# RWKV-7 value stores of a hybrid decoder step: issued from GpSimd's queue instead of ScalarE's

## The chip, the core and the metric

The kernel runs on one core of one Trainium2 chip. The metric is the device time of one execution in microseconds (us), the median of several runs. The core's engines are TensorE (PE in the profile; its weight loads are PEld), VectorE (DVE), ScalarE (ACT), GpSimd (POOL) and SyncE (SP). Each works through its own instructions in order; waits between them are semaphores. A DMA is issued by an instruction in the queue of one of these engines; ACTq and SPq in the profile are the instructions of ScalarE's and SyncE's sequencers.

## The reference: one step of a two-layer decoder

1024 prompt tokens and 8 sequences of 8 sample tokens (1088 columns in all, model width 1024) go through two layers. Layer 0 mixes tokens by stick-breaking attention, layer 1 by RWKV-7 with 16 heads of 64; each mixer is followed by a squared-ReLU MLP of width 4096. Cut to the part that matters here:

```python
r = xr @ w_r
k = xk @ w_k
v = xv @ w_v
...
def step(S, inp):
    r_t, w_t, k_t, v_t, kk_t, b_t = inp
    sa = jnp.einsum('bhij,bhj->bhi', S, kk_t)
    S = (S * w_t[:, :, None, :] - sa[..., None] * b_t[:, :, None, :]
         + v_t[..., None] * k_t[:, :, None, :])
    return S, jnp.einsum('bhij,bhj->bhi', S, r_t)
```

`v` is needed twice: with features first (for the bonus term) and, for the chunked form of the recurrence, with tokens first, per head and chunk of 64 tokens.

## The kernel before

Activations lie with the 1024 features on partitions, in eight tiles of 128, and tokens along the free dimension. The tokens are cut into two halves (`HALF`): the first has 576 prompt tokens, in matmul chunks of 288, the second 448 prompt and 64 sample tokens in one chunk of 512. `dense` (L354 to L368) multiplies in three passes for precision: weights and activations are split into a high and a low part (`weight`, L350 and L351; `split`), and per tile of weights three matmuls (L364 to L366) add into one PSUM bank. PE does this during almost the whole kernel.

Beside this main line runs background work: attention, then the RWKV units (`rw_units`, `rw_unit`: per eighth of the features, decay, key normalisation, and the small matrices of all chunks) and then the RWKV chains (`rw_chain`), which walk the recurrence. The background is a Python generator, and `step` (L186), called after each three matmuls, takes pieces of it at a set rate. `beside` adds a second such stream (for example the loads and splits of the next projection). So the program order interleaves main line and background, and the framework (`TileContext` with `schedule_with_timeline_sim=True`) fixes each engine's final order when the program is built, from a planner's model of costs. The framework also gives the DMAs their landing semaphores.

The value projection of layer 1 is the third `dense_to` of `mixer_in` (L1685). For each of eight feature tiles m:

- `dense` makes 128 features of v for the half, and `self.copy` (L132 on ScalarE or L134 on VectorE, alternating by `flip`) brings them from PSUM (`dq`) to SBUF (`dn`).
- ScalarE issues the store of `dn` to `s_vt` (L1017).
- `rw_value` (L1021) transposes `dn` on PE (L140) into PSUM (`vq`) with tokens on partitions, copies it to SBUF (`vt`, again L132 or L134), and stores it to the scratch `s_v` in pieces: for each head of the pair and each group of 64 partitions one DMA. A block of 512 tokens gives four stores of 64 KB, the last 64 tokens of the first half two stores of 16 KB. That is 6 x 8 = 48 stores in the first half and 4 x 8 = 32 in the second, all issued from ScalarE's queue.

`dn`, `vt` and many other tiles share the six buffers of the pool `n`; a buffer can be written again when the last DMA that reads it has landed.

During the two value stages the background is `rw_unit`. On ScalarE it has, among others, activations (L1093 `s` and `a`, L1106 `G`, L1107 `Gi`, L1117 `t`), copies (L1169 `L`, L1184 `S`) and the DMA issues of its results to `s_st`, `s_p` and `s_l` (L1124, L1144, L1173, L1174, L1187, L1188, L1189). On GpSimd it has L1105 (memset of `G`), L1108 (`gend`), L1119 and L1120 (`a`), and L1130 (`AR`, second part), which L1188 stores. Every second `split` puts its low part on GpSimd too (L311: `xlo`, `slo`), and `residual` adds the sample columns there (L385). `rw_chain` reads `s_v` back on SyncE's queue (L1274), `rw_samples` at L1389. SyncE issues all weight loads of these stages (L347) and most other loads. GpSimd issues no DMA in this kernel.

Of the kernel before, what the change touches and what calls it, by code (L numbers as in the profile page):

```python
# [106 lines left out]
class Kern:  # L107
# [913 lines left out]
    def rw_value(self, m, pt, t, tmp, ps):  # L1021

        nc = self.nc
        for w0 in range(0, pt.W, 512):
            n = min(128, pt.W - w0)
            nw = min(512, pt.W - w0) // n
            q = ps.tile([128, 512], F32, tag="dps", name="vq")
            for i in range(nw):
                self.transpose(q[:n, 128 * i:128 * i + 128], t[:, w0 + 128 * i:w0 + 128 * i + n])
            o = tmp.tile([128, 4, 128], F32, tag="n", name="vt")[:n, :nw, :]  # L1030
            self.copy(o, q[:n, :128 * nw].rearrange("p (w c) -> p w c", w=nw))
            c = pt.c0 + w0 // 64
            for hd in range(2):
                for p in range(n // 64):
                    nc.scalar.dma_start(self.s_v[m, hd][:, c + p:c + p + 2 * nw - 1:2, :],
                                      o[64 * p:64 * p + 64, :, 64 * hd:64 * hd + 64])

    def rw_keys(self, m, pt, k, pp, ps):
# [747 lines left out]
```

## Time and profile before

| | |
|---|---|
| time, median of 3 runs | 3655.77 us (3653.04 to 3656.8) |
| profiled execution | 3661.88 us |
| its span, first to last instruction | 3660.2 us |
| mean granted PE clock | 0.972 |
| value stage of the first half, s_v issues | 1585.0 to 1712.9 us |
| value stage of the second half, s_v issues | 2448.0 to 2546.5 us |

The profile is one execution. A row of the waits view names who waited and for whom, then the total in us, the times and the longest. A timeline row has the start, the length, engine, line, operation, output and inputs, and in brackets how long the engine had been idle and what ended it. In the table by stretch each engine has its busy time and its number of instructions; the last columns are the granted PE clock, the busy share of the DMA engines and what they moved. In the chain of waits, a row of DMA is the time from a transfer's issue to its landing.

### The profile page before, as it was taken

How to read it: one execution, taken by the hardware profiler on the slowest of the kernel's cores; microseconds unless marked ns; L12 is line 12 of the kernel's file. 1: busy time of each engine (PE TensorE's matmuls, PEld its weight loads, DVE VectorE, ACT ScalarE, POOL GpSimd, SP SyncE). 2: the span in 40 equal slices, each digit the busy share in tenths (PEclk: the TensorE clock that was granted, in tenths of full speed). 3: DMA queues.
4: the chain of work that ended last, by engine and by line, in shares of the span. 5: the costliest groups of instructions: out<-in, count | busy, mean ns of one | idle time of the engine just before them, and what ended most of it. 6: DMA issues, size and time to landing. Idle time of an engine off the chain costs nothing.

```text
span 3660.2 us, 71034 instructions
## 1 busy us (share of the span) xinstructions
PE 3490.5 (95%) x26360; PEld 2764.7 (76%) x26360; DVE 2328.6 (64%) x4718; ACT 1601.2 (44%) x3341; POOL 669.3 (18%) x1180
## 2 busy tenths in 40 slices
PE   8999999899999998998899998998899999989998
PEld 6976667778888875876677776666798888868886
DVE  4457788785554555778855556766984666655444
ACT  4345566663333335644334445644433444433332
POOL 1223333230000001121312113121100111121111
PEclk9999999999999999999899998999999999999999
DMA  7475653319887785667354345667444444433332
GB/s 257 141 242 190 213 168 131 88 50 337 337 295 265 277 311 162 209 201 218 95 149 139 121 148 164 188 193 234 120 129 136 140 137 124 120 114 118 94 93 84
DMA packets 433003, 634.45 MB, mean 173 GB/s; under 512 B 144337, under 2 KB 244562, under 8 KB 432658
## 3 DMA queue, kind: packets, MB, share of 16 engines
q1 hardware_dynamic: 369394, 532.90, 45.1%
q10 hardware_dynamic: 63264, 97.02, 7.9%
q8 instruction: 209, 3.42, 0.4%
q14 instruction: 136, 1.11, 0.1%
HBM read 523.76 MB, written 106.01 MB: 172 GB/s over the span
## 4 chain that ended last, share of the span: by engine, by line
PE 44%; DVE 5%; DMA 3%; issue 1%; POOL 1%; ACT 1%; SPq 1%; ACTq 0%; DVEq 0%; POOLq 0%
PE dq L364 12%; PE dq L365 12%; PE dq L366 12%; PE qc L1335 1%; PE qc L1325 1%; PE qc L1344 1%; DMA s_v<-vt 1%; PE yq L1492 1%; DMA st<-s_st 0%; DVE lxn L1218 0%; PE qc L1339 0%; DVE wl L351 0%; DVE tm L1216 0%; PE s L1152 0%; PE qc L1348 0%
## 5 line engine op out<-in xcount | busy, mean ns | idle before, releaser
L350 ACT CAST wh<-wst 128x512 fp32r<-128x512 f32 (+1 forms) x512 | 424.6, 834 | 720.5 <-PE dq L365 606.3
L364 PE MATMUL dq<-hhi,wh 128*128 128x288 f32 (+1 forms) x2112 | 709.5, 337 | 11.2 <-ACT hhi L132 7.8
L365 PE MATMUL dq<-hlo,wh 128*128 128x288 f32 (+1 forms) x2112 | 703.6, 333 | 9.6 <-DVE hlo L332 9.6
L366 PE MATMUL dq<-hhi,wl 128*128 128x288 f32 (+1 forms) x2112 | 704.6, 334 | 0.2 <-DVE wl L351 0.2
L351 DVE TENSOR_TENSOR wl<-wst,wh 128x512 fp32r<-128x512 f32 (+1 forms) x512 | 499.4, 976 | 253.9 <-ACT wh L350 229.3
L364 PE MATMUL dq<-uh,wh 128*128 128x288 f32 (+1 forms) x1536 | 506.9, 335 | 2.9 <-DVE x L379 1.4
L365 PE MATMUL dq<-ul,wh 128*128 128x288 f32 (+1 forms) x1536 | 508.2, 331 | 0.0
L366 PE MATMUL dq<-uh,wl 128*128 128x288 f32 (+1 forms) x1536 | 505.5, 331 | 0.0
L364 PEld LDWEIGHTS dq<-hhi,wh 128*128 128x128 f32 x2112 | 399.9, 190 | 63.3 <-issue 20.4
L365 PEld LDWEIGHTS dq<-hlo,wh 128*128 128x128 f32 x2112 | 400.1, 189 | 49.3 <-issue 10.9
L366 PEld LDWEIGHTS dq<-hhi,wl 128*128 128x128 f32 x2112 | 399.7, 189 | 42.8 <-issue 12.3
L379 DVE SCALAR_TENSOR_TENSOR x<-dq,mod,x 128x288 f32<-128x288 f32 (+1 forms) x432 | 245.5, 569 | 231.4 <-PE dq L366 228.4
L364 PEld LDWEIGHTS dq<-uh,wh 128*128 128x128 f32 x1536 | 287.6, 188 | 52.5 <-issue 15.9
L554 DVE TENSOR_TENSOR_SCAN prod<-prod 128x256 f32<-128x256 f32 (+5 forms) x264 | 240.7, 913 | 121.6 <-ACT prod L545 86.8
L366 PEld LDWEIGHTS dq<-uh,wl 128*128 128x128 f32 x1536 | 288.0, 188 | 28.1 <-issue 4.2
L365 PEld LDWEIGHTS dq<-ul,wh 128*128 128x128 f32 x1536 | 288.3, 188 | 26.8 <-issue 5.3
L385 POOL TENSOR_TENSOR x<-x,rs 128x64 f32<-128x64 f32 x144 | 120.8, 839 | 605.1 <-DVE rs L382 591.4
L364 PE MATMUL dq<-xhi,wh 128*128 128x288 f32 (+1 forms) x576 | 204.5, 355 | 8.4 <-ACT xhi L132 5.8
L365 PE MATMUL dq<-xlo,wh 128*128 128x288 f32 (+1 forms) x576 | 199.0, 345 | 1.0 <-DVE xlo L311 0.9
L366 PE MATMUL dq<-xhi,wl 128*128 128x288 f32 (+1 forms) x576 | 197.6, 343 | 0.0
L555 DVE TENSOR_TENSOR beta<-beta,prod 128x256 f32<-128x256 f32 (+5 forms) x264 | 140.4, 535 | 29.5 <-POOL beta L600 9.0
L478 ACT CAST uh<-ut 128x288 fp32r<-128x288 f32 (+1 forms) x192 | 94.8, 495 | 131.3 <-DVE ut L476 130.5
(300 smaller groups left out, 6113.4 us busy)
## 6 DMA issues: line engine op xcount, KB each, us to landing
pagek<-cache_kT SPq DMA_DIRECT2D x128, 512.0 KB
pagev<-cache_v SPq DMA_DIRECT2D x128, 512.0 KB
adaw<-ada_w SPq DMA_DIRECT2D x192, 256.0 KB
wst<-w_up SPq DMA_DIRECT2D x96, 512.0 KB
wst<-w_down SPq DMA_DIRECT2D x192, 256.0 KB
st<-s_st SPq DMA_DIRECT2D x40, 672.0 KB
wst<-sb_w_qkv SPq DMA_DIRECT2D x48, 512.0 KB
wst<-w_up ACTq DMA_DIRECT2D x32, 512.0 KB
```

Source lines behind the costliest of these rows:

```text
L350: nc.scalar.copy(wh, st)
L351: nc.vector.tensor_sub(wl, st, wh.bitcast(F32))
L364: nc.tensor.matmul(q, wh[:, k, :], h, start=k == 0, stop=False)
L365: nc.tensor.matmul(q, wh[:, k, :], l, start=False, stop=False)
L366: nc.tensor.matmul(q, wl[:, k, :], h, start=False, stop=k == kt - 1)
L379: nc.vector.scalar_tensor_tensor(xs, q[:, :np_], g, xs, ALU.mult, ALU.add)
L385: nc.gpsimd.tensor_add(xv, xv, t)
L478: nc.scalar.copy(a, t[:, :n])
L554: nc.vector.tensor_tensor_scan(r, r, r, 1.0 if carry is None else carry, ALU.mult, ALU.bypass)
L555: nc.vector.tensor_mul(beta[:, :w], beta[:, :w], p[:, 1:w + 1])
L1325: nc.tensor.matmul(qc[R[hd], 0:64], st[:, hd, cc, :], hv[hd][:, cc, :], start=True, stop=True)
L1335: nc.tensor.matmul(qc[r, 64:128], tt[r, cc, :], xs[r, :], start=True, stop=True)
```

## The change

The stores of `vt` to `s_v` in `rw_value` are issued from GpSimd's queue instead of ScalarE's. Their number, sizes and addresses are the same, and nothing else in the source changes.

```diff
             c = pt.c0 + w0 // 64
             for hd in range(2):
                 for p in range(n // 64):
-                    nc.scalar.dma_start(self.s_v[m, hd][:, c + p:c + p + 2 * nw - 1:2, :],
+                    nc.gpsimd.dma_start(self.s_v[m, hd][:, c + p:c + p + 2 * nw - 1:2, :],
                                       o[64 * p:64 * p + 64, :, 64 * hd:64 * hd + 64])
```

## The prediction

> **What bounds the kernel now.** I read the page's first part, then a table of busy time by stretch, then the waits of the two stretches that hold the moved stores, then the timeline and the chain of waits inside them.
>
> ```profile
> span 3660.2 us, 71034 instructions
> PE 3490.5 (95%) x26360; PEld 2764.7 (76%) x26360; DVE 2328.6 (64%) x4718; ACT 1601.2 (44%) x3341; POOL 669.3 (18%) x1180
> s_v<-vt ACTq DMA_DIRECT2D x64, 64.0 KB
> s_v<-vt ACTq DMA_DIRECT2D x16, 16.0 KB
> ```
>
> TensorE is busy 95% of the span, so over the whole kernel only PE's idle time and its clock can be won; ScalarE, whose queue the change relieves, looks idle more than half the time. But the change touches 80 stores only, and where they are is what counts:
>
> ```profile
> L1035 ACTq DMA_DIRECT2D s_v<-vt x48: 476/618/1890, 1585.0 to 1712.9; - x48
> L1035 ACTq DMA_DIRECT2D s_v<-vt x32: 591/624/940, 2448.0 to 2546.5; - x32
> ```
>
> 48 lie between 1585 and 1713 us (the value projection of the first half), 32 between 2448 and 2547 us (the second half). The table by stretch sets these two stages beside the stages just ahead of them (columns: length, PE, PEld, DVE, ACT, POOL busy with counts, PE clock, DMA share, GB/s):
>
> ```profile
> 1480.00:1575.00 95.00, 90.72 (x734) 75.02 (x734) 67.36 (x126) 52.87 (x100) 16.10 (x15) 0.97 0.63 205
> 1575.00:1720.00 145.00, 121.89 (x815) 96.48 (x810) 113.51 (x271) 57.82 (x118) 26.94 (x26) 0.91 0.71 216
> 2360.00:2445.00 85.00, 82.55 (x545) 57.03 (x545) 61.69 (x132) 46.15 (x85) 18.20 (x24) 1.00 0.59 192
> 2445.00:2550.00 105.00, 89.35 (x476) 61.59 (x475) 67.06 (x136) 39.11 (x73) 20.45 (x28) 0.90 0.75 229
> ```
>
> These are the weak places of the kernel: PE is idle 145 - 121.9 = 23.1 us in the first and 105 - 89.4 = 15.6 us in the second, against 4.3 and 2.4 us in the stages before, and its granted clock is 0.91 and 0.90 against 0.97 and 1.00. So at most about 39 us of idle time and some clock are at stake, 1% of the kernel. The waits of the two stretches (total, times, longest) say who holds PE up. First stretch:
>
> ```profile
> PE vq L140 <- ACT dn L132: 16.6, 3, 7.2
> ACT s L1093 <- DMA s_v<-vt: 3.8, 1, 3.8
> ```
>
> Second stretch:
>
> ```profile
> ACT S L1184 <- DMA s_v<-vt: 8.7, 2, 4.6
> PE vq L140 <- ACT dn L132: 7.9, 3, 4.6
> ACT dn L132 <- DMA s_v<-vt: 5.6, 1, 5.6
> ACT shi L132 <- DMA s_v<-vt: 3.4, 1, 3.4
> ```
>
> The largest PE wait in both is the same: the transposes (vq) wait for ScalarE's copy of the projection out of PSUM (dn), 16.6 + 7.9 = 24.5 us of the 39. And ScalarE's computations wait for landings of s_v stores, 3.8 + 8.7 + 5.6 + 3.4 = 21.5 us, though none of them (s, S, dn, shi) reads or writes s_v. The wait is that of a store issue standing ahead of them in ScalarE's in-order queue. The chain of waits shows how such an issue comes to wait:
>
> ```profile
> 1663.47 4.10 DMA s_v<-vt
> 1667.67 0.59 ACTq L1035
> ```
>
> The store issued at 1663.47 lands 4.10 us later, and only then does the next issue of L1035 start. The framework gives the loads and stores of SyncE and ScalarE a few landing semaphores in turn, and an issue waits until the last transfer on its own one has landed. ScalarE's timeline at this place, then PE's:
>
> ```profile
> 1667.56 0.50 ACT L1093 ACTIVATE s<-lq,hwa 128x288 f32<-128x288 f32 x1 [3.84 <-DMA s_v<-vt]
> 1672.53 0.39 ACT L132 COPY dn<-dq 128x288 f32<-128x288 f32 x1
> ```
>
> ```profile
> 1672.97 0.47 PE L140 MATMUL vq<-cst,dn 128*128 128x128 f32 x1 [7.15 <-ACT dn L132]
> ```
>
> ScalarE stood 3.84 us behind the store, worked through what had piled up, and made dn at 1672.53; PE had waited 7.15 us.
>
> **What is removed.** 80 issues leave ScalarE's sequencer: 48 x 0.618 + 32 x 0.624 = 29.7 + 20.0 = 49.6 us of issue time, and with them the waits for landing semaphores. Issue time runs beside ScalarE's arithmetic as long as the queue keeps ahead, so I count it at nothing and count only waits that reached PE. The gap at 1672.97 gives back the 3.84 us; the other 3.3 us were work and DVE waits that stay. The other large gaps, in PE's timeline:
>
> ```profile
> 1705.98 0.90 PE L140 MATMUL vq<-cst,dn 128*128 128x128 f32 x3 [6.54 <-ACT dn L132]
> ```
>
> ```profile
> 2494.52 0.79 PE L140 MATMUL vq<-cst,dn 128*128 128x128 f32 x3 [2.96 <-ACT dn L132]
> ```
>
> ```profile
> 2530.98 0.69 PE L140 MATMUL vq<-cst,dn 128*128 128x128 f32 x2 [4.65 <-ACT dn L132]
> ```
>
> Ahead of them on ScalarE stand these rows of its timeline:
>
> ```profile
> 1702.34 1.25 ACTq L1035 DMA_DIRECT2D s_v<-vt  x2
> 1703.63 0.87 ACT L1117 ACTIVATE t<-a,omka,hka 128x576 f32<-128x576 f32 x1 [2.23 <-DMA s_st<-S]
> 2489.36 0.43 ACT L1184 COPY S<-bkq 128x320 f32<-128x320 f32 x1 [4.64 <-DMA s_v<-vt]
> 2529.18 0.69 ACT L1093 ACTIVATE s<-lq,hwa 128x512 f32<-128x512 f32 x1 [4.02 <-DMA s_st<-S]
> ```
>
> At 1703.63 ScalarE was held 2.23 us with two of the moved issues directly ahead: I count 2 us of the 6.54. At 2489.36 it was held 4.64 us by an s_v landing, more than the 2.96 us PE gap behind it: all 2.96. At 2529.18 it was held 4.02 us, put down to a store of S, but the chain of waits runs there through an s_v store that took longest of all:
>
> ```profile
> 2522.98 5.95 DMA s_v<-vt
> ```
>
> so I count 4.0 of 4.65. Sum of the idle time: 3.84 + 2 + 2.96 + 4.0 = 12.8 us, a third of the 39.
>
> The clock: had PE run at the clock of the stages ahead, the two stages would need 121.9 x (1 - 0.91/0.97) = 7.5 and 89.4 x (1 - 0.90/1.00) = 8.9 us less. With a third to a half of the idle time gone I take under half of it, 6 us.
>
> **What is added.** GpSimd issues the 80 stores, in order among its own work. No DMA in this trace is issued from GpSimd, so the price of one issue must be bounded. From below: the ScalarE issue of the same store, 0.62 us. From above: a small GpSimd operation at its most stretched, 4.43 us in the first of these rows.
>
> ```profile
> L1108 POOL COPY gend<-G x16: 184/270/4432, 1478.1 to 2668.2; 128x9 f32<-128x9 f32 x8, 128x7 f32<-128x7 f32 x8
> L1130 POOL TENSOR_TENSOR AR<-r,G x16: 1038/1287/2018, 1478.2 to 2668.4; 128x576 f32<-128x576 f32 x8, 128x448 f32<-128x448 f32 x8
> L385 POOL TENSOR_TENSOR x<-x,rs x144: 314/702/2874, 1719.2 to 3645.5; 128x64 f32<-128x64 f32 x144
> POOL a L1119 <- ACT t L1117: 71.8, 4, 21.8
> ```
>
> I take 1.3 us, the median of an ordinary GpSimd operation here (L1130), nearer the lower end. Then GpSimd's busy time rises by 48 x 1.3 = 62 us to 89 of 145 us in the first stage and by 32 x 1.3 = 42 us to 62 of 105 us in the second: still under two thirds. The cover is its idle time, 118 and 85 us; the last row shows it waiting 71.8 us in the first stage for ScalarE alone. A burst of six stores is 7.8 us, of four 5.2 us. Queued behind a burst are the operations of the background units, L1119, L1130, L1120, and slo; L1130 is the sharp one, since ScalarE's issue at L1188 stores its output (AR) and holds up ScalarE's queue in the old way:
>
> ```profile
> 1639.93 1.28 POOL L1130 TENSOR_TENSOR AR<-r,G 128x576 f32<-128x576 f32 x1
> 1641.24 0.34 ACTq L1188 DMA_DIRECT2D s_st<-AR  x1
> ```
>
> L1188 starts 0.03 us after L1130 ends, so there is no slack. This happens once per unit, eight times in the two stages; I charge half a microsecond each for a store or two ahead of it, 4 us in all. The buffer of vt comes free when the last store lands, as before; now six issues take 7.8 us, while before, in the first batch, the stores ran from 1585.0 to 1595.1. I charge nothing. Should each issue cost more than about 2.5 us, this cover is gone (third rival).
>
> SyncE's queue issues nothing more or less; it shares the landing semaphores, so its loads wait for fewer slow stores, for which I count nothing. The data is read back at the earliest at 1845.7 us for the first half:
>
> ```profile
> L1274 SPq DMA_DIRECT2D hv<-s_v x96: 444/566/1190, 1845.7 to 3149.9; - x96
> ```
>
> so a store that lands some us later hurts no reader. The planner that fixes each engine's order sees other costs and may order the neighbourhood anew; I give that no sign.
>
> The sum: -12.8 - 6 + 4 = -14.8 us, call it -15. The profiled execution took 3661.9 us (span 3660.2), 6.1 us over the median 3655.8; I carry the difference over to the median: 3655.8 - 15 = 3641 us.
>
> A rule of the Trainium skill speaks against the change. "SBUF — State Buffer", section "SBUF: two separate sides", says that a DMA issued from GpSimd has its descriptors written by GpSimd's cores, and that VectorE, while it runs an operation in a two-port mode, locks GpSimd out of the port they share. The page gives about 620 ns alone and 3100 ns beside such a copy; by its slow figure, as an estimate, the 80 stores would take 248 us of GpSimd instead of 104. The trace agrees in kind: the same tiny copy at L1108 takes 184 ns at best and 4432 ns at worst. That no run so far shows it for a DMA is why it stands as a rival and not in the sum.
>
> **The rivals.** *First, no change.* The PE gaps stay because dn is late for other reasons: ScalarE also waits for its 100-odd other issues of these stages and for DVE, which is 78% busy in the first one. For it: the 2.23 and 4.02 us waits are put down to s_st, not s_v. Then only the direct share at 1672.97 comes back, 3.8 us, and the 4 us charge eats it: 3656 us. Chance 0.22.
>
> *Second, more than forecast.* The stages come up to the standard of those ahead: idle 23.1 + 15.6 falls to the 4.3 and 2.4 us there, with half the clock: 32 + 8 = 40 us less, 3616 us. For it: all of ScalarE's s_v waits add up to 21.5 us and every semaphore turns over sooner. Against it: DVE gaps show next. Chance 0.10.
>
> *Third, slower.* GpSimd becomes the bound of the two stages, since DVE stretches its issues. From (145 - 26.9)/48 = 2.46 us per issue on in the first stage, and (105 - 20.5)/32 = 2.64 in the second, the vt buffers are not emptied in time, and the next projection waits for a buffer. At 2.87 us, the worst of L385: 48 x 2.87 + 26.9 - 145 = 20 us, and 32 x 2.87 + 20.5 - 105 = 7 us: 27 us slower, 3683 us. Against it: the medians of GpSimd's rows are far below their worst. Chance 0.18, smaller losses below this point included.
>
> **How the numbers follow.** My forecast, 3641 us, has 0.50. About 0.2%, 7.3 us, is what a measurement of this kernel can tell from no change. The forecast's own spread (no clock gain and 4.43 us where bursts meet L1130, or the whole 24.5 us wait regained) goes from -25 to -6 us, so a little of it falls within 0.2%: faster 0.46 + 0.10 = 0.56, same 0.04 + 0.22 = 0.26, slower 0.18. The range runs from 3620, near the second rival, to 3668 us, part of the way to the third.
>
> **What would show it.** In the new profile: no s_v in ScalarE's waits; PE's wait for dn under 14 us in the two stages together, from 24.5; PE's clock there above 0.92; about 1.3 us between neighbouring s_v issues on GpSimd. Wrong, if GpSimd is busy nearly the whole of these stages, if ScalarE's issues of AR wait several us for L1130, or if PE's waits move to DVE with the stages no shorter.

## The result, and the profile after

| | before | after |
|---|---|---|
| median of 4 runs each | 3654.4 us (3651.2 to 3656.8) | 3683.6 us (3681.6 to 3685.2) |
| ratio, 95% interval | | 1.0072 [1.0057, 1.0087] |
| profiled execution, its span | 3661.9, 3660.2 us | 3684.5, 3682.8 us |
| mean granted PE clock | 0.972 | 0.967 |

The change makes the kernel 0.7% slower; the forecast was 0.4% faster. First the page of after:

```profile
span 3682.8 us, 71083 instructions
PE 3496.7 (95%) x26360; PEld 2775.9 (75%) x26360; DVE 2326.9 (63%) x4718; ACT 1604.8 (44%) x3344; POOL 709.6 (19%) x1260
q0 software_dynamic: 2560, 4.46, 0.5%
```

GpSimd has 80 instructions more and 40 us more busy time, and a new DMA queue carries the 4.46 MB. PE's matmuls are the same in number and busy 6 us longer; the other 16 of the 22.6 us are idle time. The moved line in after, first half and second half, and how long its transfers took to land:

```profile
L1035 POOL DMA_DIRECT2D s_v<-vt x48: 533/620/803, 1579.3 to 1690.9; - x48
DMA to landing us min/median/max: 2.1/4.1/7.0
L1035 POOL DMA_DIRECT2D s_v<-vt x32: 620/622/695, 2437.4 to 2534.5; - x32
```

One issue takes 0.62 us on GpSimd in the median, what it took on ScalarE, and 0.803 us at the most. The stages seem shorter than before: 111.6 us from first to last store against 127.9, and 97.1 against 98.5. The same stretches by engine in after, the stage ahead of each first:

```profile
1475.00:1570.00 95.00, 91.29 (x736) 75.41 (x737) 67.52 (x127) 52.84 (x101) 16.50 (x15) 0.96 0.63 204
1570.00:1700.00 130.00, 114.39 (x758) 92.97 (x758) 96.97 (x228) 52.75 (x105) 49.50 (x69) 0.93 0.72 226
2350.00:2435.00 85.00, 84.52 (x576) 58.90 (x574) 53.35 (x124) 47.18 (x94) 16.92 (x19) 1.00 0.58 188
2435.00:2537.00 102.00, 87.59 (x452) 59.91 (x451) 65.43 (x128) 38.92 (x68) 37.87 (x60) 0.88 0.71 226
```

PE is idle 15.6 of 130 us in the first stage (23.1 of 145 before), and GpSimd is busy 49.5 of 130 us: no engine has become a bound. PE's waits for dn in after's first stage, then in its second, are for other copies than before:

```profile
PE vq L140 <- DVE dn L134: 12.9, 4, 4.2
PE vq L140 <- DVE dn L134: 1.7, 1, 1.7
PE vq L140 <- ACT dn L132: 0.7, 2, 0.5
```

In before the transposes waited for ScalarE's copies; here they wait mostly for VectorE's. That is another order of work. PE's order is the same in the two traces up to its 12,531st matmul, at 1588 us in before, and from there to 3250 us 9,826 places of the order hold a matmul of another line.

To see where the time goes I cut both traces at the same points of the main line: the dense matmuls (L364 to L366) are 13,824 in the same order in every version, so the start of the n-th one is a milestone. The value projection of the first half is 5952 to 6336 by this count, that of the second half 8448 to 8640. From the traces, for each stretch: length in us, PE's idle time in it, and the number of background matmuls run in it.

```
dense matmuls   before: us  idle  backgr.   after: us  idle  backgr.   after - before
0-6144              1604.5  51.1   5604       1598.5  49.1   5596        -6.0
6144-6528            140.7  28.7    308        133.1  27.3    262        -7.6
6528-6912            108.5   3.8    204        128.6   7.8    324       +20.1
6912-7104             59.0   0.0    198         53.5   0.1    132        -5.5
7104-9216            717.0  44.4   2598        707.9  46.0   2538        -9.1
9216-9408             30.0   0.0     56         45.8   4.9     68       +15.8
9408-12096           523.6   5.7   2048        521.5   3.8   2068        -2.1
12096-12288           54.3   6.6      0         72.0  16.9     28       +17.7
12288-end            374.7   8.7      0        375.4   8.5      0        +0.7
```

The first row lies almost wholly ahead of the change (it ends with half of the first value projection) and varies between executions: a second profile of before has 1601.8. The other half is in 6144-6528, the second value projection in 7104-9216. Both stretches are shorter in after and run 46 and 60 background matmuls fewer: in each half one RWKV unit runs later. The work put off comes back behind them: +20.1 us in 6528-6912, +15.8 in 9216-9408, +17.7 in 12096-12288. Without the first row the sum is +30.0 us.

Work that is only moved takes its time once, wherever it runs: behind the first row there are 5,412 background matmuls in before and 5,420 in after. Of the 30.0 us, 17.4 are more idle time of PE, 10.3 of them in 12096-12288, 4.9 in 9216-9408 and 4.0 in 6528-6912. For the other 12.6 us PE is busy longer; its granted clock in these three stretches, in the same order, was 0.91, 0.81 and 0.88, against 0.97, 1.00 and 0.95 in before. The sizes vary too: in a second profile of the changed kernel, at 3675.8 us the fastest of its five runs (gpsimd_new_order below), they are 17.3, 11.0 and 17.3 us longer than in before, and the sum is some 20 us.

In 9216-9408 it is the last RWKV unit that comes late. GpSimd's copies of these units, in before and in after:

```profile
L1108 POOL COPY gend<-G x4: 190/342/492, 2561.2 to 2668.2; 128x7 f32<-128x7 f32 x4
```

```profile
L1108 POOL COPY gend<-G x4: 192/222/335, 2577.0 to 2690.2; 128x7 f32<-128x7 f32 x4
```

The last one starts 22 us later. In 12096-12288 the main line must wait for all background (`self.until(lambda: False)`, L1650) and then loads the recurrence's result `y` of the second half. The stores of `y` in before, then in after, and behind them after's longest PE gap of the whole trace:

```profile
L1502 SPq DMA_DIRECT2D s_y<-yT x32: 319/368/1176, 1960.5 to 3218.5; - x32
```

```profile
L1502 SPq DMA_DIRECT2D s_y<-yT x32: 319/366/430, 1957.1 to 3245.0; - x32
```

```profile
3255.78 0.80 PE L364 MATMUL dq<-shi,wh 128*128 128x512 f32 x1 [9.72 <-ACT shi L132]
```

The last store of `y` is 26.5 us later, and PE stands 9.7 us for the first tile of it.

### The profile page after: what moved, and what is told of

The parts are those of the page before. It is cut to its first block, busy times and chain, and to the rows that moved or that the text cites. A ratio compares the mean times of both kernels' runs of the same rounds, so it can differ in the third digit from the quotient of the medians.

```text
span 3682.8 us, 71083 instructions
## 1 busy us (share of the span) xinstructions
PE 3496.7 (95%) x26360; PEld 2775.9 (75%) x26360; DVE 2326.9 (63%) x4718; ACT 1604.8 (44%) x3344; POOL 709.6 (19%) x1260
## 3 DMA queue, kind: packets, MB, share of 16 engines
q0 software_dynamic: 2560, 4.46, 0.5%
## 5 line engine op out<-in xcount | busy, mean ns | idle before, releaser
L364 PE MATMUL dq<-hhi,wh 128*128 128x288 f32 (+1 forms) x2112 | 711.5, 338 | 11.6 <-ACT hhi L132 8.9
L366 PE MATMUL dq<-hhi,wl 128*128 128x288 f32 (+1 forms) x2112 | 705.4, 334 | 4.3 <-DVE wl L351 4.2
L364 PE MATMUL dq<-uh,wh 128*128 128x288 f32 (+1 forms) x1536 | 510.9, 338 | 2.0 <-ACT uh L478 0.6
L366 PE MATMUL dq<-uh,wl 128*128 128x288 f32 (+1 forms) x1536 | 510.7, 334 | 0.0
L364 PEld LDWEIGHTS dq<-hhi,wh 128*128 128x128 f32 x2112 | 401.2, 190 | 64.2 <-issue 19.8
L366 PEld LDWEIGHTS dq<-hhi,wl 128*128 128x128 f32 x2112 | 400.9, 190 | 46.0 <-issue 11.3
L364 PEld LDWEIGHTS dq<-uh,wh 128*128 128x128 f32 x1536 | 291.1, 190 | 54.4 <-issue 17.1
L366 PEld LDWEIGHTS dq<-uh,wl 128*128 128x128 f32 x1536 | 291.3, 190 | 29.0 <-issue 4.6
L364 PE MATMUL dq<-xhi,wh 128*128 128x288 f32 (+1 forms) x576 | 205.3, 357 | 7.0 <-ACT xhi L132 6.5
L366 PE MATMUL dq<-xhi,wl 128*128 128x288 f32 (+1 forms) x576 | 198.5, 345 | 0.0
```

What stands on the lines that cost most here:

```text
L364: nc.tensor.matmul(q, wh[:, k, :], h, start=k == 0, stop=False)
L366: nc.tensor.matmul(q, wl[:, k, :], h, start=False, stop=k == kt - 1)
```

## Experiments

The theory: the change does two things. It moves 80 issues to another queue, which costs or gives little, and it makes the planner order all engines anew, which costs about 30 us. The first rival is the prediction's own kind: the move itself costs the time, by new waits in GpSimd's or ScalarE's queue. Two further rivals came up on the way: that the whole loss is the exposed tail of the background (12096-12288), and that one bad stage makes it.

### The move and the order, each alone

To hold an order fixed, the last thing the program does is to chain each engine's instructions in the order that another version has, by dependencies that order without a semaphore (shortened: the list of names is kept packed in the kernel):

```diff
         Kern(tc, I, O).run()
+        keep_order(tc, nc, ['PE', 'DVE', 'Activation', 'Pool', 'SP'])
+
+def keep_order(tc, nc, engines):
...
+    for e in engines:
+        last = None
+        for n in names[e]:
+            i = traced.get(n)
+            if i is None or i.engine != getattr(mybir.EngineType, e):
+                continue
+            if last is not None:
+                tc.add_manual_dep(i, last.name, info, reason="the other kernel's order")
+            last = i
```

A store that sits on another queue than in the version whose order is kept is left to the planner, which places it among the fixed ones. In gpsimd_old_order the stores are GpSimd's and the order is before's; in scalar_new_order the stores are ScalarE's and the order is after's.

> The changed kernel (s_v stores on GpSimd), but every engine's other instructions are kept in the order that they had in the kernel before. Theory 'order': moving the stores in itself saves what the two stages won in the changed profile (12 to 20 us), and the 29 us are the price of the new order that the planner made; then this runs at 3635 to 3643 us, 12 to 20 us faster than before. Theory 'queue': stores issued from GpSimd cost time themselves, by late landings or by their semaphores, whatever the order; then it stays near 3684 us.

> The kernel before (s_v stores on ScalarE), but every engine's other instructions in the order of the changed kernel. Theory 'order': the new order costs about 45 us wherever the stores are, so it is slower than the changed kernel too: 3695 to 3705 us. Theory 'queue': without GpSimd's stores it is back at 3654 us, give or take 5.

> The kernel of gpsimd_old_order again, on one chip with the changed kernel, since its profiled execution was 14 us faster than that of before and its timed runs 2 us. If the stores' move is worth my 15 us by itself: 3640 us. If it is worth nothing that can be measured: 3650 to 3657 us.

> The changed kernel itself, beside the others on one chip: 3680 to 3687 us by every theory.

| stores on | order of | median us | before on the same chip | ratio, 95% interval |
|---|---|---|---|---|
| GpSimd | before | 3654.6 | 3656.7 | 0.9995 [0.9983, 1.0008] |
| GpSimd | before, again | 3653.2 | 3656.7 | 0.9994 [0.9984, 1.0005] |
| ScalarE | after | 3696.5 | 3656.7 | 1.0116 [1.0091, 1.0141] |
| GpSimd | after (the changed kernel) | 3684.1 | 3656.7 | 1.0075 [1.0062, 1.0088] |

With the old order the move costs nothing that can be measured (-2 and -3 us, both intervals hold 1); the gain of 12 to 20 us that theory 'order' expected is not there either. With the old place of the stores the new order alone costs 40 us. Within the new order the move gives 12 us back (3696.5 to 3684.1). So the loss is the order's, and the rival that the move costs the time falls. No run holds before's own order with the stores on ScalarE, to price the chain itself; but in the stretches that hold no store of v gpsimd_old_order takes as long as before within 0.3 us (6528-6912, 6912-7104, 9216-9408 and 12096-12288 in the table of the next section) or less (9408-12096). The new order is worse for ScalarE's queue in particular; its waits in the first stage and, the last row, in the second, with ScalarE's stores in after's order:

```profile
ACT dn L132 <- DMA s_v<-vt: 8.5, 2, 5.0
ACT shi L132 <- DMA s_v<-vt: 7.8, 2, 5.1
ACT wh L350 <- DMA s_v<-vt: 6.7, 2, 5.0
```

By name these waits are absent from after. That they are the source of the 12 us is argued, not tested.

### Where in the order the loss is

There are four more orders, all with GpSimd's stores. Two leave part of the order free to the planner: before's order only from the end of the first value stage on (gpsimd_old_order_late), or only up to there (gpsimd_old_order_early). Two join the orders of before and after at the 7104th dense matmul (some 1950 us): new_order_then_old and old_order_then_new. Their edit is the list of names that the chain goes through.

> The changed kernel, with the order of before kept only for what comes after the first half's value stage; up to there the planner is free. Theory 'order', if the loss lies in the order after the stages (the changed profile falls behind at about 1880, 2680 and 3240 us of its span): 3633 to 3645 us. If the loss comes from the order within the first stage: about 3684. Theory 'queue': 3684.

> The changed kernel, with the order of before kept only up to the end of the first half's value stage; after it the planner is free and makes a third order, unlike that of before and that of the changed kernel. Theory 'order': the time is whatever this new order is worth, somewhere from 3635 to 3700 us, and not the 3684 of the changed kernel by rule. Theory 'queue': 3684.

> The changed kernel; all engines in the new order up to the place where the main line has issued 7104 of its 13824 dense matmuls (about 1951 us of the span), and in the order of before from there. Background work that the new order has put off in the first value stage has been made up by then; in the profiles the changed kernel loses about 10 us up to here. Theory 'put-off background': about 10 us over gpsimd_old_order. Theory 'tail alone' (the loss is made only where the main line waits for the last chains, after 3220 us): no more than gpsimd_old_order, and if the first value stage's gain is real, 10 us less.

> The changed kernel; the order of before up to the same place, the new order from there. Theory 'put-off background': the rest of the loss, about 18 to 20 us over gpsimd_old_order, in two places: the last unit of the second half (2660 to 2690 us) and the last chains (after 3220 us). Theory 'tail alone': the whole loss, about 29 us over gpsimd_old_order.

| version | median us | ratio, 95% interval |
|---|---|---|
| gpsimd_old_order_late | 3671.0 | 1.0041 [1.0026, 1.0056] |
| gpsimd_old_order_early | 3670.8 | 1.0044 [1.0028, 1.0061] |
| new_order_then_old | 3664.7 | 1.0019 [1.0008, 1.0031] |
| old_order_then_new | 3675.8 | 1.0050 [1.0037, 1.0063] |

Length of each stretch in us, from the traces:

```
                       6144-6528 6528-6912 6912-7104 7104-9216 9216-9408 9408-12096 12096-12288
before                     140.7     108.5      59.0     717.0      30.0      523.6        54.3
gpsimd_old_order           139.1     108.6      59.0     715.0      29.7      519.4        54.6
after                      133.1     128.6      53.5     707.9      45.8      521.5        72.0
new_order_then_old         132.2     128.4      53.8     712.9      29.7      521.4        54.6
old_order_then_new         142.6     108.5      58.6     709.8      40.6      523.6        71.4
gpsimd_old_order_late      150.8     108.5      59.0     719.6      29.7      521.1        54.6
gpsimd_old_order_early     139.3     106.4      52.0     708.5      43.1      539.1        54.6
```

The halves add up: against gpsimd_old_order on the same chip (3653.2 us) new_order_then_old costs 11.5 us and old_order_then_new 22.5, together 34.0, and after costs 3684.1 - 3653.2 = 30.9; each has an interval of some 4 to 5 us to both sides. Each half's loss shows in its own stretches and goes when that half is undone. So it is neither the tail alone, which would have left nothing in the first half, nor one stage. That the put-off work is the mechanism rests on these stretches; no run put back that work alone.

The other two are a third and a fourth order, and gpsimd_old_order_late lies at neither of the times that were expected of it. With the first stage free the planner loses 10 us in 6144-6528 (150.8, PE idle 36.9 us), and loses them behind the value projection; with the rest free it gains 18 us on before between 6528 and 9216 and loses 29 behind that. Each freed plan tried here is slower than before's, each in another place.

### Does one small move do it too?

last_four_on_gpsimd is before with 4 of the 80 stores on GpSimd, the last ones of the second half, and a free plan:

```diff
-                    nc.scalar.dma_start(self.s_v[m, hd][:, c + p:c + p + 2 * nw - 1:2, :],
-                                      o[64 * p:64 * p + 64, :, 64 * hd:64 * hd + 64])
+                    q = nc.gpsimd if pt.o and m == 7 else nc.scalar
+                    q.dma_start(self.s_v[m, hd][:, c + p:c + p + 2 * nw - 1:2, :],
+                                o[64 * p:64 * p + 64, :, 64 * hd:64 * hd + 64])
```

> The kernel before with only 4 of the 80 stores moved to GpSimd (the last feature tile of the second half), order left to the planner, which makes a fourth order: it differs from that of before in more lines of PE's list than the middle order above. Theory 'the order is a draw': the time is not in proportion to the stores moved; anything from 3645 to 3700 us, and more than 7 us away from 3656 is likely. Theory 'cost per store': 4/80 of 29 us, that is 1.5 us: 3658 us.

3670.8 us against 3658.7: 1.0036 [1.0022, 1.0050]. Four issues of 0.62 us cost 12 us; the trace has most of it in 9408-12096 (533.8 us against 523.6), from some 2700 us on, while before's last store is at 2546.5. The size of an edit says little about the size of the re-ordering that it sets off.

### Why the move itself gives so little

The forecast gave the move 15 us; it gives 2 or 3, if anything. To be sure that differences between profiles are not those between executions, before was profiled once more, and to see whether it is ScalarE's relief or GpSimd's queue that matters, the stores went to SyncE's queue in before's order:

```diff
-                    nc.scalar.dma_start(self.s_v[m, hd][:, c + p:c + p + 2 * nw - 1:2, :],
+                    nc.sync.dma_start(self.s_v[m, hd][:, c + p:c + p + 2 * nw - 1:2, :],
```

> The kernel before once more, for a second profile of it: its timed runs lie between 3648 and 3666 us, the profiled one was at 3662 and that of gpsimd_old_order at 3648. By either theory 3648 to 3666 us. If the waits for dn in the two value stages are again near 24 us, their fall to 15.5 in gpsimd_old_order is the stores' doing; if they are near 15, it was the execution's.

> The 80 stores on SyncE's queue, every engine's other instructions in the order of before. ScalarE is relieved as in gpsimd_old_order, but the stores stay among the landing semaphores of the other two queues and stand in front of SyncE's loads. If the relief of ScalarE is what saved PE's waits for dn, and GpSimd's queue costs nothing: about 3654 us, like gpsimd_old_order. If GpSimd's queue ate a gain of some 10 us: 3643 us. If stores in front of loads hurt: 3660 us and more.

before_profile took 3657.7 us in its one run. In it PE's waits for ScalarE's dn are, in the first and the second stage:

```profile
PE vq L140 <- ACT dn L132: 14.2, 3, 6.7
PE vq L140 <- ACT dn L132: 5.5, 3, 3.4
```

19.7 us where the first profile had 24.5: a fifth of the term that the forecast was built on comes and goes between two executions of one kernel. SyncE's queue: 3659.8 us against 3658.7, 1.0010 [1.0002, 1.0019]. ScalarE's relief does not pay there either, and a wait for s_v still stands in ScalarE's list, though none is issued from it:

```profile
ACT s L1093 <- DMA s_v<-vt: 4.2, 1, 4.2
```

That is the sharing of landing semaphores between SyncE's and ScalarE's transfers that the prediction described: in the traces the DMAs of both queues signal the same eight semaphores. Those of GpSimd signal eight others, and with its queue no such wait is left.

Since the order is the same, one can look at the same PE instruction in each trace. PE's idle time in us just ahead of the four waits for dn that the prediction named, and ahead of the two that grew:

```
start in before              before  again   gpsimd_old_order  again
1672.97 vq <- ACT dn           7.15   6.75         5.43         6.38
1705.98 vq <- ACT dn           6.54   4.56         4.42         4.42
2494.52 vq <- ACT dn           2.96   1.81         2.08         1.23
2530.98 vq <- ACT dn           4.65   3.45         0.96         0.96
2516.51 s  <- ACT L            0.59   0.59         2.86         2.87
2539.21 kb <- DVE kv           0.00   0.00         2.55         2.25
both stages, all gaps          39.9   34.2         35.4         35.8
```

The four fell by 6.0 us in the mean of two profiles each (18.9 to 12.9), not by 12.8. And 4.7 of the 6.0 are taken again by two waits close by that were not there before. In gpsimd_old_order's timeline of PE:

```profile
2505.43 0.79 PE L1152 MATMUL s<-AR,BK 64*128 64x128 f32 x2 [2.86 <-ACT L L1169]
2518.91 0.65 PE L140 MATMUL vq<-cst,dn 128*128 128x128 f32 x4 [0.96 <-ACT dn L132]
2527.61 0.50 PE L1064 MATMUL kb<-kv,cst 32*128 32x128 f32 x8 [2.55 <-DVE kv L1060]
2528.35 0.92 PE L140 MATMUL vq<-cst,dn 128*128 128x128 f32 x4 [0.23 <-ACT dn L132]
```

The two value projections together (5952 to 6336 and 8448 to 8640) take 252.1 and 245.2 us in the two profiles of before, and 242.0 and 242.5 in those of gpsimd_old_order. That is 6.4 us less in the mean, where the two profiles of before are 6.9 us apart; the runs show 2 to 3.

### Are the two new waits GpSimd's doing?

In sync_old_order, with the same order of the other instructions, the four waits for dn are 4.91, 4.42, 2.06 and 1.64 us, 13.0 in all, and the two new ones 0.56 and 0.00. So the relief of ScalarE is what shortens the four, on whichever of the two queues the stores go, and the two new waits come with GpSimd's queue. Less idle time did not make that kernel faster: its two value projections take 251.3 us in the one profile.

ScalarE has a new wait in that stage, in gpsimd_old_order:

```profile
ACT dn L132 <- POOL AR L1133: 5.3, 1, 5.3
ACT shi L132 <- POOL AR L1133: 4.1, 1, 4.1
```

GpSimd's timeline shows why (same kernel):

```profile
2522.06 1.04 POOL L1130 TENSOR_TENSOR AR<-r,G 128x448 f32<-128x448 f32 x1
2523.05 2.51 POOL L1035 DMA_DIRECT2D s_v<-vt  x4
2525.57 1.27 POOL L1120 TENSOR_TENSOR a<-a,Gi 128x512 f32<-128x512 f32 x1
2526.78 0.27 POOL L1113 COPY gend<-Gs 128x8 f32<-128x8 f32 x1
2527.02 0.30 POOL L1133 TENSOR_TENSOR AR<-r,Gs 128x64 f32<-128x64 f32 x1
```

Four issues stand between the two parts of AR, and ScalarE's store of AR (L1188) waits for the second. In ar_ahead_of_stores the two bursts of the second half that stood so come behind L1133; GpSimd's order, cut to one of them:

```diff
 L1130 TENSOR_TENSOR AR<-r,G 128x448
-L1035 DMA s_v<-vt 64x4x64 x4
 L1113 COPY gend<-Gs 128x8
 L1133 TENSOR_TENSOR AR<-r,Gs 128x64
+L1035 DMA s_v<-vt 64x4x64 x4
```

> GpSimd's stores with the order of before, but in the second half the two bursts of four stores that stood between GpSimd's two parts of AR (L1130 and L1133) come after the second part; the order of all other instructions is that of gpsimd_old_order. What is open: PE's idle time ahead of the four waits for dn fell from 21.3 and 16.6 us (two profiles of before) to 12.9 and 13.0 us (two profiles of gpsimd_old_order), but the two stages together lost only some 1.5 us of idle time, and the time only 2 to 3 us. Theory A (a new wait of the move's own making): ScalarE's store of AR (L1188) now stands behind four GpSimd issues, 2.5 us each time; ScalarE waited 5.3 us and 4.1 us for L1133 there, where before waited nothing. Then ScalarE's waits for POOL AR in 2430 to 2555 us fall from 9.4 us to about 4, and the new PE gaps of 2.9 us (s waiting for ScalarE's L) and 2.5 us (kb waiting for kv) shrink with it: 3 to 5 us, 3649 to 3651 against 3656, a ratio of 0.9982 to 0.9987. Theory B (the next wait was there anyway): PE had only 0.2 us of idle time behind that wait for dn, so the wait is hidden; the two new gaps are VectorE's chain (kv, S), which comes last once dn is earlier. Then ScalarE's waits for AR fall as in A, the gaps of 2.9 and 2.5 us stay within half a microsecond, and the time is that of gpsimd_old_order, 0.9990 to 1.0000.

3651.7 us against 3658.2: 0.9985 [0.9976, 0.9993], the only version that is faster than before, and so than both kernels. The waits in ScalarE's list and then the two PE gaps, in its profile:

```profile
ACT dn L132 <- POOL AR L1133: 3.8, 1, 3.8
ACT shi L132 <- POOL AR L1133: 1.5, 1, 1.5
```

```profile
2518.92 0.49 PE L1152 MATMUL s<-AR,BK 64*128 64x128 f32 x2 [1.91 <-ACT L L1169]
2537.24 0.50 PE L1064 MATMUL kb<-kv,cst 32*128 32x128 f32 x8 [1.48 <-DVE kv L1060]
```

ScalarE's wait for L1133 fell from 9.4 to 5.3 us and the two gaps from 5.4 to 3.4. The time lies where theory A put it, and the gaps moved by more than B allowed; sync_old_order speaks against B too: PE's waits for dn are as short there, and the gaps are absent. But 3.4 us of them stay. All of PE's gaps in the second stage are 14.8 us, against 17.7 and 17.3 in gpsimd_old_order; in the first, where nothing was changed, they are 20.3 against 17.7 and 18.5, so that such a difference can also come from one execution to the next. And the interval overlaps those of gpsimd_old_order (0.9995 and 0.9994). That the move with this repair is a little faster than before is shown; how much of it the two bursts are worth stays open.

## Why the prediction was wrong

**The failed step** is the one sentence on the planner: it "may order the neighbourhood anew; I give that no sign". It ordered far more than the neighbourhood, from 1588 to 3250 us, and the sign was a loss of some 30 us with GpSimd's stores and 40 with ScalarE's. No row of before's profile shows what a new plan will be, but that a plan exists, that it sees the queue of each DMA, and that it orders the whole program was known. It deserved a rival with a chance of its own and a width of tens of microseconds. The second failure is a size: the idle time to be won.

**What is removed.** By name ScalarE's waits for landings of s_v (21.5 us) are gone, as forecast. But the five ScalarE instructions that had them in before, where they stood 21.6 us (19.5 in its second profile), still stand 17.3 and 17.1 us in the two profiles of gpsimd_old_order, now put down to PE and to GpSimd's AR. A wait that is put down to one landing is not won when that landing goes.

The first term, 3.84 us at 1667.56, was misread. The store issued at 1663.47 landed 4.10 us later, at 1667.57, when `s` had already started. What stood ahead of `s` were issues in ScalarE's queue, in before:

```profile
1663.47 1.59 ACTq L1035 DMA_DIRECT2D s_v<-vt  x1
1665.15 2.36 ACTq L1187 DMA_DIRECT2D s_st<-S  x2
```

Only the first of the three is moved, 1.59 us; the other two stay. It was issue time that held ScalarE, the very thing that the prediction counted at nothing. The four terms of the sum, 3.84, 2, 2.96 and 4.0 us, came to 1.0, 1.1, 0.7 and 3.1, together 6.0 instead of 12.8, and the two new waits took 4.7 of them.

**The clock** was to give 6 us. In the stages it was 0.91 and 0.90, and 0.89 and 0.93 in the two profiles of before, 0.93 and 0.92, and 0.92 and 0.92 in those of gpsimd_old_order. In the two value projections PE is busy 210.6 and 210.7 us in before and 206.3 and 206.4 in gpsimd_old_order, 4.3 us less for the same matmuls. But directly behind them (6336-6528 and 8640-9216) it is busy 3.9 us longer in the mean (179.2 and 181.7, then 183.0 and 185.8). With the same matmuls the value projections take 209.9 us of PE in ar_ahead_of_stores and 217.5 in sync_old_order, so a lasting gain can't be told from the spread.

**What is added.** One issue costs 0.62 us, the lower bound, not 1.3. Instead of 4 us for GpSimd's stores ahead of AR, ScalarE waited 9.4 us for it in the second half; behind the longest of these waits PE was idle 0.23 us. The reason named was right. Most of that wait was hidden, but the two new waits of PE, 4.7 us, came with the stores on GpSimd's queue too.

**GpSimd's DMAs beside VectorE.** In after the 80 issues take 533 to 803 ns, in a first stage in which VectorE is busy 97 of 130 us, and their transfers land within 7.0 us. The Trainium skill ("SBUF — State Buffer", section "SBUF: two separate sides") says that a copy by VectorE from SBUF to SBUF keeps GpSimd from writing the descriptors of its DMAs, and gives 620 ns for a DMA alone and 3100 ns beside such a copy. No issue here is stretched like that, but the runs do not test that figure: 56 of after's 80 issues have a VectorE operation beside them, and none of these is a copy from SBUF to SBUF (the copies are `vt` and `gt`, out of PSUM). The GpSimd copy that the prediction set beside it (L1108, 4432 ns at worst) ran next to tensor-tensor operations of VectorE, L1216, L1218 and L1058 to L1060, in before; operations of the same lines ran beside issues in after and stretched none.

**The rivals.** "No change" (3656 us) is what the move alone does, within its interval. "Slower, GpSimd becomes the bound" named 3683 us, the measured time, by a mechanism that did not happen. The two stages with the move alone, in gpsimd_old_order:

```profile
1570.00:1715.00 145.00, 127.30 (x865) 101.11 (x864) 118.04 (x278) 60.62 (x122) 57.07 (x75) 0.93 0.72 224
2435.00:2540.00 105.00, 88.83 (x479) 61.56 (x477) 69.18 (x137) 39.35 (x74) 39.65 (x60) 0.92 0.74 234
```

GpSimd is busy 57 of 145 and 40 of 105 us. A right number is no evidence for its story.

**What would show it.** No s_v in ScalarE's waits: right. PE's wait for dn under 14 us: 15.3 in after (12.9 + 1.7 + 0.7), so not quite; and on VectorE's copies now, since the order is another. The clock above 0.92: 0.93 and 0.88. About 1.3 us from issue to issue: 0.62. The stages no shorter would be a sign of error, said the prediction; they were shorter, and the kernel was slower, because the work had moved out of them. A check by stage is no check unless the work of the stage is the same.

## What to carry to other kernels

When a planner orders the program, a change of one queue is two changes: measure the edit with the old order held fixed, and the new order with the old edit, before explaining either. Compare traces at milestones of the main line and count what ran between them; a stage that got shorter may only have put work off. And before a wait is booked as a gain, look at the same instruction in a second profile of the same kernel, and at what is late directly behind it. Look as well at what stood in the engine's queue during the wait: the landing that the profile names need not be what held it.

## What the runs showed of the hardware

A DMA issue on GpSimd took 0.62 us in the median (0.53 to 0.81 in most traces, 0.92 at the most), the same as on ScalarE (0.62) and SyncE (0.61), next to a VectorE that was 81% busy; bursts of four took 2.5 us and most of six 3.6. DMA issues in ScalarE's own queue held up its arithmetic: 3.84 us in before at 1667.56, while one issue took 1.59 and two more 2.36 us. GpSimd's transfers take no part in the waits that ScalarE's issues have for earlier transfers, while SyncE's do (4.2 us for one of them).
